# Other start addresses for TensorE's operands, and another order of two token tiles, in a hybrid decoder layer

## The chip, the cores and the metric

The kernel runs on one core of a Trainium2 chip. The metric is the device time of one execution in microseconds (us), the median of the runs.

## The reference

One layer, in float32, on 256 tokens with 16 learned meta tokens put before them (272 rows in all), model width 4096:

```python
h = rmsnorm(x, norm_g)
p = h @ w_in                                   # 4096 -> 16384
q, k, v, g_attn, b, c, hc, z = split(p)        # 8 x 2048 = 16 heads or groups of 128
o = stick_breaking_attention(q, k, v)          # 16 heads, strictly causal
o = group_rmsnorm(o * silu(g_attn))
y = b * short_conv(c * hc)                     # 3 taps
y = group_rmsnorm(y * silu(z))
out = rmsnorm(x + concat([o, y]) @ w_out)      # 4096 -> 4096, meta rows dropped
```

The two large products, with `w_in` (4096 x 16384) and `w_out` (4096 x 4096), make up nearly all of the arithmetic.

## The kernel before, in words

**Split products.** Every float32 operand of the two large products is kept as a pair of float32r values: a rounded part (`h`) and the rest (`lo`). A product is h times h, h times lo and lo times h. ScalarE makes `h` (a cast, L84), VectorE makes `lo` (a subtraction, L85).

**Weights.** They arrive in chunks of 128 partitions x 1024 columns (4 KB a partition), one DMA each on SyncE's queue, into four rotating buffers `raw`; each chunk is split into one of four `wh` and one of four `wl`, up to three steps before TensorE uses it. A chunk holds eight slices of 128 columns for `w_in`, two of 512 or four of 256 for `w_out`.

**Input projection, 128 blocks of 128 output columns.** x stands transposed in `xs`, one tile of four k (k counts 32 groups of 128 channels): for each k a row of 272 tokens of the rounded part and a row of 272 of the rest, one behind the other. The weights' slice is the stationary operand (128 x 128), x is the moving one, and 32 k add up in one PSUM bank. There are three kinds of block, each with its own loop body:

- fused blocks (q, attention gate, b, z; 64 of them): per k a pair, L216 (`lo` with 256 columns of the rounded x) and L218 (`h` with both rows of x, 2 x 256 = 512 columns; the first k has it under L215). The meta tokens are skipped, so a row is read from its 16th token on.
- k and v (32 blocks): per k a trio, L222, L223, L224, each of 272 columns, from the row's beginning; L223 moves the second row, the other two the first.
- c and h of the convolution (32 blocks): the same trio with 258 columns, from the row's 14th token on.

The first unit (16 steps) works on four blocks in turn, two k of each in a step; all later steps work on eight k of one block.

**Mixing.** Attention, convolution, gates and norms of each unit run on VectorE and ScalarE in tasks some steps later; TensorE gets a few small products between blocks. The result, one of 32 mixed channel groups, is split into `mixh` and `mixl` (256 tokens each).

**Output projection.** Here the mixed channels are the stationary operand (128 channels x 128 tokens, so two token tiles) and the weights move: seven blocks of 512 columns with 16 chunks each, then two of 256 with eight. Per channel group m and token tile t there is a trio L471, L472, L473. Each token tile has a PSUM bank of its own. When a block is complete, VectorE and ScalarE add the residual, take squares and multiply by the final gain, per token tile. The last block does token tile 0 first and tile 1 after it; four of its chunks are kept split in tiles `kh` and `kl`.

**Where operands begin.** The pools are filled in a fixed order, so a tile's first byte within its partition follows from the sizes of what lies before it. Counted modulo 256 bytes, before the change the weights (`raw`, `wh`, `wl`) begin at 64 and every slice of them too, the mixed channels at 224, the kept chunks at 224. A row of x is 272 x 4 = 1088 bytes and a k is 2176 bytes, 8.5 times 256, so that x begins at alternating places: in a fused block the first row is read from 32 or 160 (the second from 96 or 224), in k and v blocks the first from 224 or 96 (the second from 32 or 160), in convolution blocks the first from 24 or 152 (the second from 88 or 216); the first of each pair of numbers belongs to an even k, the other to an odd one.

Of the kernel before, what the change touches and what calls it, by code (L numbers as in the profile page):

```python
# [8 lines left out]
F32 = mybir.dt.float32  # L9
F32R = mybir.dt.float32r  # L10
# [5 lines left out]
P = 128  # L16
# [3 lines left out]
META = 16  # L20
L = SEQ + META
HEADS = 16
UNITS = 32
# [3 lines left out]

# Reciprocal square root: an exponent-halving seed, one tuned Newton step, one cubic step.
SEED = float(0x5F1FFFF9)
NA = 2.38924456  # L30
NB = 0.703952253
RS = -0.375 * NB

# Matrix products before the first data; the step at which the rows' statistics begin.
WARM = 10
S0 = 7

# Columns of the packed parameters.
G0, CW0, AG0, CG0, NPAR = 0, 32, 80, 96, 112
# [3 lines left out]
def kernel(ctx, tc, xt, xin, par, fg, w1, w2, out):  # L43
    nc = tc.nc

    const = ctx.enter_context(tc.tile_pool(name="const", bufs=1))
    wp = ctx.enter_context(tc.tile_pool(name="wp", bufs=4))
    wk = ctx.enter_context(tc.tile_pool(name="wk", bufs=1))
    pp = ctx.enter_context(tc.tile_pool(name="pp", bufs=8, space=bass.MemoryType.PSUM))

    def bank(nm):
        return pp.tile([P, 512], F32, tag="bank", name=nm)

    # The tensor engine's clock rises while it works.
    ones = const.tile([P, P], F32, name="ones")
# [7 lines left out]

    # ------------------------------------------------------------ weights
    raws, splits = {}, {}
# [21 lines left out]

    # ------------------------------------------------------------ constants
    ones_r = const.tile([P, P], F32R, name="ones_r")
    nc.scalar.copy(out=ones_r, in_=ones)  # L90
    # Attention weights [query, key]: the second query tile's key tile 1, key tile 0 of both query
    # tiles, then the last 16 keys of each, 32 columns apart.
    za = const.tile([P, 3 * P + 64], F32, name="za")
    nc.vector.memset(za[:, 3 * P:], 0.0)
    # Transposed, [key, query]: key tile 1 (16 queries of the first tile, the second), key tile 0.
    at = const.tile([P, META + 3 * P], F32, name="at")
# [5 lines left out]
    for off in (META, 144 + META + P):  # L102
        # Column c of the diagonal block is a key before query p where c < p.
        nc.gpsimd.affine_select(out=zmask[:, off:off + P], in_=zmask[:, off:off + P],
                                pattern=[[-1, P]], compare_op=ALU.is_gt, fill=NEG,
                                base=0, channel_multiplier=1)
    one = const.tile([P, 1], F32, name="one")
# [5 lines left out]
    def rsqrt_raw(src, n, eps, nm):  # L113
        """u with rsqrt(src + eps) = RS * u."""
        x = wk.tile([P, 272], F32, tag="rx", name=f"rx{nm}", bufs=1)[:, :n]
        y = wk.tile([P, 272], F32, tag="ry", name=f"ry{nm}", bufs=1)[:, :n]
        t = wk.tile([P, 272], F32, tag="rt", name=f"rt{nm}", bufs=1)[:, :n]
        v = nc.vector
        v.tensor_scalar(out=x, in0=src, scalar1=eps, scalar2=None, op0=ALU.add)  # L119
        v.tensor_scalar(out=y.bitcast(I32), in0=x.bitcast(I32), scalar1=-0.5, scalar2=SEED,  # L120
                        op0=ALU.mult, op1=ALU.add)
        v.tensor_tensor(out=t, in0=y, in1=y, op=ALU.mult)
        v.tensor_tensor(out=t, in0=t, in1=x, op=ALU.mult)
        v.scalar_tensor_tensor(out=y, in0=t, scalar=-NA, in1=y, op0=ALU.add, op1=ALU.mult)
        v.scalar_tensor_tensor(out=t, in0=y, scalar=NB * NB, in1=y, op0=ALU.mult, op1=ALU.mult)
        v.tensor_tensor(out=t, in0=t, in1=x, op=ALU.mult)
        v.scalar_tensor_tensor(out=t, in0=t, scalar=-10.0 / 3.0, in1=t, op0=ALU.add, op1=ALU.mult)
        v.scalar_tensor_tensor(out=y, in0=t, scalar=5.0, in1=y, op0=ALU.add, op1=ALU.mult)
        return y

    # ------------------------------------------------------------ mixed channels, split
    mixh, mixl = [], []

    def open_mix():
        sctx.close()
        mixp = ctx.enter_context(tc.tile_pool(name="mixp", bufs=1))
        mixh.extend(mixp.tile([P, SEQ], F32R, name=f"mixh{m}") for m in range(UNITS))
        mixl.extend(mixp.tile([P, SEQ], F32R, name=f"mixl{m}") for m in range(UNITS))

    # ------------------------------------------------------------ steps over weight chunks  # L140
    # Unit 0: two k of all four blocks in a step. Other blocks: eight k of one block.
    steps = [(0, kc) for kc in range(16)]
    for b in range(4, 128):
        steps.extend((b, kc) for kc in range(4))
    n1 = len(steps)
    # w_out: seven blocks of 512 columns, then two of 256.
    for nb in range(7):
# [23 lines left out]
    xp = xctx.enter_context(tc.tile_pool(name="xp", bufs=1, side="right"))  # L171
    xs = [xp.tile([P, 4, 2, L], F32R, name=f"xs{j}") for j in range(8)]
    sctx = ExitStack()
# [8 lines left out]
    def prep_x(k):  # L182
        j, kk = k // 4, k % 4
        g = pt[:, G0 + k:G0 + k + 1]
        nc.scalar.mul(out=xs[j][:, kk, 0, :], in_=xr[j][:, kk, :], mul=g)
        nc.vector.scalar_tensor_tensor(out=xs[j][:, kk, 1, :], in0=xr[j][:, kk, :], scalar=g,
                                       in1=xs[j][:, kk, 0, :].bitcast(F32),
                                       op0=ALU.mult, op1=ALU.subtract)
# [19 lines left out]
    def mm_k(b, k, h, lo):  # L208
        """One k of a block of w_in."""
        ps = psum[b]  # L210
        x = xs[k // 4][:, k % 4]
        first, last = k == 0, k == KC - 1
        if b % 8 in (0, 3, 6, 7):
            if first:
                nc.tensor.matmul(out=ps, lhsT=h, rhs=x[:, :, META:], start=True, stop=False)  # L215
            nc.tensor.matmul(out=ps[:, :SEQ], lhsT=lo, rhs=x[:, 0, META:], start=False, stop=False)  # L216
            if not first:
                nc.tensor.matmul(out=ps, lhsT=h, rhs=x[:, :, META:], start=False, stop=last)  # L218
        else:
            s = 0 if b % 8 < 4 else META - 2  # L220
            o = ps[:, s:L]
            nc.tensor.matmul(out=o, lhsT=h, rhs=x[:, 0, s:], start=first, stop=False)  # L222
            nc.tensor.matmul(out=o, lhsT=h, rhs=x[:, 1, s:], start=False, stop=False)  # L223
            nc.tensor.matmul(out=o, lhsT=lo, rhs=x[:, 0, s:], start=False, stop=last)  # L224
# [15 lines left out]
    def blocks(dst, src, n):  # L240
        """n [128, 128] transposes from one with its 32 x 32 blocks transposed in place."""
        d = dst.rearrange("p (c x) -> p c x", c=n)
        s = src.rearrange("p (c x) -> p c x", c=n)
        for i in range(4):
            for j in range(4):
                o = d[32 * j:32 * j + 32, :, 32 * i:32 * i + 32]
                x = s[32 * i:32 * i + 32, :, 32 * j:32 * j + 32]
                if (i + j) % 2:
                    nc.vector.tensor_copy(out=o, in_=x)
                else:  # L250
                    nc.scalar.copy(out=o, in_=x)  # L251

    def fold(ps, r, nm, tag, width=SEQ):
        """Both halves of a fused block, times the rows' scale."""
        t = wk.tile([P, width], F32, tag=tag, name=f"{tag}{nm}")[:, :SEQ]
        nc.scalar.copy(out=t, in_=ps[:, SEQ:])
        nc.vector.tensor_tensor(out=t, in0=ps[:, :SEQ], in1=t, op=ALU.add)
        nc.vector.tensor_tensor(out=t, in0=t, in1=r, op=ALU.mult)
        return t
# [29 lines left out]
    def head_block(b, e):  # L289
        u = b // 4  # L290
        h = u // 2
# [5 lines left out]
        elif kind == 1:  # L297
# [32 lines left out]
            def trans():  # L330
                y = wk.tile([P, 448], F32, tag="zl", name=f"ya{h}")
                nc.vector.transpose(out=y, in_=za)  # L332
                blocks(at[:, META:], y[:, :3 * P], 3)
                # Only the last 16 queries of a tile see its last 16 keys.
                nc.vector.tensor_copy(out=at[:META, :META], in_=y[96:96 + META, 400:416])
# [93 lines left out]

    # ------------------------------------------------------------ output projection  # L430
    res, fgs, acc, sqs = [], {}, [], []
# [23 lines left out]
    def mm_out(ci, ts):  # L455
        b, kc = steps[ci]
        wh, wl = splits[ci]
        _, n = cols(b)
        nm = 1024 // n
        if kc == 0:  # L460
            for t in ts:
                psum[b, t] = bank(f"mo{b}_{t}")
        for kk in range(nm):
            m = nm * kc + kk
            h = wh[:, kk * n:(kk + 1) * n]
            lo = wl[:, kk * n:(kk + 1) * n]
            for t in ts:
                o = psum[b, t][:, :n]
# [42 lines left out]

    # ------------------------------------------------------------ the program
    load_x(0, 1)
# [21 lines left out]
    for i in range(1 - SPLITS, n_steps):  # L535
        # The last block's kept chunks are split up to four steps earlier.
        ahead = min(4, max(0, i - (n_steps - 16) + 5))
# [95 lines left out]
```

## Time and profile before

| | |
|---|---|
| median of 3 runs | 1894.76 us (1894.72 to 1895.06) |
| span of the profiled execution, first to last instruction | 1893.8 us |
| TensorE (PE) busy | 1880.2 us, 99% |
| weight loads (PEld) busy | 1721.8 us, 91% |
| VectorE (DVE) busy | 1226.0 us, 65% |
| ScalarE (ACT) busy | 952.7 us, 50% |
| DMA queue of the kernel, share of 16 engines | 56.7% |

The span stands for the profiled execution's own time; around it lies the launch, and the median of the runs is 1.0 us above it. "Busy" is the time in which at least one instruction of the engine is under way. TensorE's matmuls are pipelined and overlap in the record, so that a full bar does not say how fast they follow each other; starts of consecutive matmuls do.

### The profile page before, as it was taken

Reading aid. Unit: us, or ns where it says so; the run is one execution under the profiler, and the core shown is the slowest. Engines: PE = TensorE matmul, PEld = TensorE weight load, DVE = VectorE, ACT = ScalarE, POOL = GpSimd, SP = SyncE. Lnnn points to the kernel's source line nnn. Section 1 sums busy time; section 2 is a strip of 40 time slices with the busy share of each in tenths; the row PEclk is TensorE's granted clock in tenths of the full one; section 3 lists DMA queues with packets and bytes.
Section 4 is the critical chain, followed back from the end, with each engine's and each line's share of the span. In section 5 each row is a group of like instructions: output and inputs, shape, how many; then the busy total and the mean of one; then the engine's idle time right before and its main releaser. Section 6 shows DMA issues by size and latency. Waiting matters only on the chain.

```text
span 1893.8 us, 30516 instructions
## 1 busy us (share of the span) xinstructions
PE 1880.2 (99%) x12214; PEld 1721.8 (91%) x12214; DVE 1226.0 (65%) x1904; ACT 952.7 (50%) x1381; POOL 0.7 (0%) x6
## 2 busy tenths in 40 slices
PE   9999999999999999999999999999999999999997
PEld 8999999999999999999999999999999988888887
DVE  8987666766666667676767676767676754555544
ACT  7665454545454545454545454545454543444433
POOL 0000000000000000000000000000000000000000
PEclk9999999999999999999999999999999999999999
DMA  8555555555555555555555555555555586665564
GB/s 307 171 178 186 171 186 172 184 172 185 172 184 173 184 173 184 173 184 173 183 174 183 175 182 175 181 175 181 176 180 176 181 288 195 193 195 192 191 191 165
DMA packets 100510, 352.53 MB, mean 186 GB/s; under 512 B 11280, under 2 KB 12560, under 8 KB 100368
## 3 DMA queue, kind: packets, MB, share of 16 engines
q1 hardware_dynamic: 100368, 350.59, 56.7%
q8 instruction: 95, 1.56, 0.4%
q14 instruction: 47, 0.39, 0.1%
HBM read 346.35 MB, written 4.19 MB: 185 GB/s over the span
## 4 chain that ended last, share of the span: by engine, by line
PE 99%; DMA 0%; DVE 0%; SPq 0%; ACT 0%; issue 0%; DVEq 0%; ACTq 0%
PE mm L218 24%; PE mm L222 13%; PE mm L223 13%; PE mm L224 13%; PE mm L216 13%; PE mo L473 6%; PE mo L472 6%; PE mo L471 6%; PE mm L215 1%; PE z L304 0%; DMA raw<-w 0%; PE po L366 0%; PE po L368 0%; PE po L367 0%; PE z L303 0%; PE ss L277 0%
## 5 line engine op out<-in xcount | busy, mean ns | idle before, releaser
L85 DVE TENSOR_TENSOR wl<-raw,wh 128x1024 fp32r<-128x1024 f32 (+1 forms) x638 | 777.4, 1219 | 452.3 <-ACT wh L84 449.0
L84 ACT CAST wh<-raw 128x1024 fp32r<-128x1024 f32 (+1 forms) x638 | 667.1, 1046 | 778.8 <-PE mm L223 331.0
L218 PE MATMUL mm<-xs,wh 128*128 128x512 f32 x1984 | 698.9, 394 | 0.0
L222 PE MATMUL mm<-xs,wh 128*128 128x258 f32 (+1 forms) x2048 | 590.5, 288 | 1.2 <-ACT wh L84 1.2
L223 PE MATMUL mm<-xs,wh 128*128 128x258 f32 (+1 forms) x2048 | 587.2, 287 | 0.0
L224 PE MATMUL mm<-xs,wl 128*128 128x258 f32 (+1 forms) x2048 | 583.4, 285 | 0.0
L216 PE MATMUL mm<-xs,wl 128*128 128x256 f32 x2048 | 563.3, 280 | 0.3 <-DVE wl L85 0.3
L218 PEld LDWEIGHTS mm<-xs,wh 128*128 128x128 f32 x1984 | 371.7, 187 | 83.9
L223 PEld LDWEIGHTS mm<-xs,wh 128*128 128x128 f32 x2048 | 387.1, 189 | 2.7
L216 PEld LDWEIGHTS mm<-xs,wl 128*128 128x128 f32 x2048 | 384.5, 188 | 4.8 <-DVE wl L85 0.7
L222 PEld LDWEIGHTS mm<-xs,wh 128*128 128x128 f32 x2048 | 384.7, 188 | 2.6 <-ACT wh L84 1.5
L224 PEld LDWEIGHTS mm<-xs,wl 128*128 128x128 f32 x2048 | 386.0, 189 | 0.2
L473 PE MATMUL mo<-wl,mixh 128*128 128x512 f32 (+1 forms) x544 | 205.7, 378 | 0.0
L472 PE MATMUL mo<-wh,mixh 128*128 128x512 f32 (+1 forms) x544 | 203.6, 374 | 0.0
L471 PE MATMUL mo<-wh,mixl 128*128 128x512 f32 (+1 forms) x544 | 202.7, 373 | 0.0
L472 PEld LDWEIGHTS mo<-wh,mixh 128*128 128x128 f32 x544 | 102.1, 188 | 21.8
L471 PEld LDWEIGHTS mo<-wh,mixl 128*128 128x128 f32 x544 | 102.2, 188 | 20.2
L473 PEld LDWEIGHTS mo<-wl,mixh 128*128 128x128 f32 x544 | 102.3, 188 | 19.3
L251 ACT COPY at<-ya 32x96 f32<-32x96 f32 x128 | 34.5, 269 | 12.2 <-DVE ya L332 10.7
L251 ACT COPY vv<-yv 32x64 f32<-32x64 f32 x128 | 31.0, 243 | 1.7
L119 DVE TENSOR_SCALAR rxm<-ss 128x256 f32<-128x256 f32 x32 | 13.6, 424 | 26.2 <-PE ss L277 26.2
L318 DVE SCALAR_TENSOR_TENSOR zs<-zm,zl 128x416 f32<-128x416 f32 x16 | 9.5, 592 | 30.5 <-ACT zl L311 30.4
(141 smaller groups left out, 907.4 us busy)
## 6 DMA issues: line engine op xcount, KB each, us to landing
raw<-w SPq DMA_DIRECT2D x638, 512.0 KB, 3.4
xr<-xt SPq DMA_DIRECT2D x15, 272.0 KB, 6.4
res<-xin SPq DMA_DIRECT2D x14, 256.0 KB, 4.9
out<-res SPq DMA_DIRECT2D x4, 512.0 KB, 3.4
fg<-fg SPq DMA_DIRECT2D x7, 256.0 KB, 4.0
out<-res SPq DMA_DIRECT2D x2, 640.0 KB, 4.8
raw<-w SPq DMA_DIRECT2D x4, 256.0 KB, 4.8
res<-xin SPq DMA_DIRECT2D x4, 128.0 KB, 4.6
```

The costliest lines, as they stand in the source:

```text
L84: nc.scalar.copy(out=h[:, c], in_=t[:, c])
L85: nc.vector.tensor_tensor(out=lo[:, c], in0=t[:, c], in1=h[:, c].bitcast(F32), op=ALU.subtract)
L215: nc.tensor.matmul(out=ps, lhsT=h, rhs=x[:, :, META:], start=True, stop=False)
L216: nc.tensor.matmul(out=ps[:, :SEQ], lhsT=lo, rhs=x[:, 0, META:], start=False, stop=False)
L218: nc.tensor.matmul(out=ps, lhsT=h, rhs=x[:, :, META:], start=False, stop=last)
L222: nc.tensor.matmul(out=o, lhsT=h, rhs=x[:, 0, s:], start=first, stop=False)
L223: nc.tensor.matmul(out=o, lhsT=h, rhs=x[:, 1, s:], start=False, stop=False)
L224: nc.tensor.matmul(out=o, lhsT=lo, rhs=x[:, 0, s:], start=False, stop=last)
L251: nc.scalar.copy(out=o, in_=x)
L471: nc.tensor.matmul(out=o, lhsT=ml, rhs=h, start=m == 0, stop=False)
L472: nc.tensor.matmul(out=o, lhsT=mh, rhs=h, start=False, stop=False)
L473: nc.tensor.matmul(out=o, lhsT=mh, rhs=lo, start=False, stop=m == UNITS - 1)
```

## The change

Five edits, in the diff below. The DMA scratch at the bottom of each partition shrinks from 16384 to 256 bytes. A row of `xs` grows from 272 to 320 elements (1280 bytes, five times 256), of which 272 are written and read as before. Three unused tiles, `pad_w`, `pad_m` and `pad_x`, shift what lies behind them. Counted modulo 256 bytes, the weights and the mixed channels now begin at 128; both rows of every k of x are read from 128 in fused blocks, from 64 in k and v blocks and from 120 in convolution blocks; the kept chunks stay at 224. In `mm_out` the loop over the token tiles stands outside the loop over a chunk's channel groups.

```diff
+XROW = 320
...
+    wp.tile([P, 16], F32, name="pad_w", bufs=1)
     pp = ctx.enter_context(tc.tile_pool(name="pp", bufs=8, space=bass.MemoryType.PSUM))
...
         mixp = ctx.enter_context(tc.tile_pool(name="mixp", bufs=1))
+        mixp.tile([P, 24], F32, name="pad_m")
...
-    xs = [xp.tile([P, 4, 2, L], F32R, name=f"xs{j}") for j in range(8)]
+    xs = [xp.tile([P, 4, 2, XROW], F32R, name=f"xs{j}") for j in range(8)]
+    xp.tile([P, 40], F32, name="pad_x")
...
-        nc.scalar.mul(out=xs[j][:, kk, 0, :], in_=xr[j][:, kk, :], mul=g)
-        nc.vector.scalar_tensor_tensor(out=xs[j][:, kk, 1, :], in0=xr[j][:, kk, :], scalar=g,
-                                       in1=xs[j][:, kk, 0, :].bitcast(F32),
+        nc.scalar.mul(out=xs[j][:, kk, 0, :L], in_=xr[j][:, kk, :], mul=g)
+        nc.vector.scalar_tensor_tensor(out=xs[j][:, kk, 1, :L], in0=xr[j][:, kk, :], scalar=g,
+                                       in1=xs[j][:, kk, 0, :L].bitcast(F32),
...
-        x = xs[k // 4][:, k % 4]
+        x = xs[k // 4][:, k % 4, :, :L]
...
-        for kk in range(nm):
-            m = nm * kc + kk
-            h = wh[:, kk * n:(kk + 1) * n]
-            lo = wl[:, kk * n:(kk + 1) * n]
-            for t in ts:
+        for t in ts:
+            for kk in range(nm):
+                m = nm * kc + kk
+                h = wh[:, kk * n:(kk + 1) * n]
+                lo = wl[:, kk * n:(kk + 1) * n]
                 o = psum[b, t][:, :n]
...
-    nc = bacc.Bacc("TRN2", target_bir_lowering=False, num_devices=1)
+    nc = bacc.Bacc("TRN2", target_bir_lowering=False, num_devices=1, dynamic_dma_scratch_size=256)
```

On TensorE only the output projection's order differs. Its first chunk stood like this before; a row names the line, the PSUM tile (`mo_0` and `mo_1` are the banks of the two token tiles), the moving weights and the stationary channels:

```order
L471 MATMUL mo_0_16171<-wh_16232,mixl_992 128x512
L472 MATMUL mo_0_16171<-wh_16232,mixh_960 128x512
L473 MATMUL mo_0_16171<-wl_16233,mixh_960 128x512
L471 MATMUL mo_1_16172<-wh_16232,mixl_992 128x512
L472 MATMUL mo_1_16172<-wh_16232,mixh_960 128x512
L473 MATMUL mo_1_16172<-wl_16233,mixh_960 128x512
L471 MATMUL mo_0_16171<-wh_16232,mixl_993 128x512
L472 MATMUL mo_0_16171<-wh_16232,mixh_961 128x512
L473 MATMUL mo_0_16171<-wl_16233,mixh_961 128x512
L471 MATMUL mo_1_16172<-wh_16232,mixl_993 128x512
```

The bank alternates after every trio. The same place after the change, on TensorE, with the lines' new numbers and the tiles' new ones:

```order
L476 MATMUL mo_0_16174<-wh_16235,mixl_995 128x512
L477 MATMUL mo_0_16174<-wh_16235,mixh_963 128x512
L478 MATMUL mo_0_16174<-wl_16236,mixh_963 128x512
L476 MATMUL mo_0_16174<-wh_16235,mixl_996 128x512
L477 MATMUL mo_0_16174<-wh_16235,mixh_964 128x512
L478 MATMUL mo_0_16174<-wl_16236,mixh_964 128x512
L476 MATMUL mo_1_16175<-wh_16235,mixl_995 128x512
L477 MATMUL mo_1_16175<-wh_16235,mixh_963 128x512
L478 MATMUL mo_1_16175<-wl_16236,mixh_963 128x512
L476 MATMUL mo_1_16175<-wh_16235,mixl_996 128x512
```

Two channel groups now follow each other in one bank before the other token tile's bank is written. All other rows of TensorE, and all rows of the other engines, keep their places.

## Rows read from the trace of the kernel before

**Rows 1.** The profile page: the span, TensorE's busy time, and the chain that ended last.

```profile
span 1893.8 us, 30516 instructions
...
PE 1880.2 (99%) x12214; PEld 1721.8 (91%) x12214; DVE 1226.0 (65%) x1904; ACT 952.7 (50%) x1381; POOL 0.7 (0%) x6
...
PE 99%; DMA 0%; DVE 0%; SPq 0%; ACT 0%; issue 0%; DVEq 0%; ACTq 0%
```

**Rows 2.** Windows: stretch, each engine's busy time and count, granted clock, DMA share, GB/s.

```profile
60.00:1548.00 1488.00, 1488.00 (x10214) 1390.22 (x10213) 1002.64 (x1639) 772.94 (x1161) 0.00 (x0) 1.00 0.56 181
```

**Rows 3.** Groups by line and shape: count | busy us, mean ns of one | idle before.

```profile
L218 PE MATMUL mm<-xs,wh 128*128 128x512 f32 x1984 | 698.9, 394 | 0.0
...
L222 PE MATMUL mm<-xs,wh 128*128 128x272 f32 x1024 | 298.7, 292 | 1.2 <-ACT wh L84 1.2
...
L222 PE MATMUL mm<-xs,wh 128*128 128x258 f32 x1024 | 291.9, 285 | 0.0
...
L471 PE MATMUL mo<-wh,mixl 128*128 128x512 f32 x448 | 175.6, 392 | 0.0
```

**Rows 4.** Timeline of TensorE, a k block: start us, duration, line; first of each trio.

```profile
496.16 0.29 PE L222 MATMUL mm<-xs,wh 128*128 128x272 f32 x1
...
496.53 0.29 PE L222 MATMUL mm<-xs,wh 128*128 128x272 f32 x1
...
496.92 0.29 PE L222 MATMUL mm<-xs,wh 128*128 128x272 f32 x1
...
497.29 0.29 PE L222 MATMUL mm<-xs,wh 128*128 128x272 f32 x1
```

**Rows 5.** The same in a convolution block: two trios, then the ninth.

```profile
450.03 0.28 PE L222 MATMUL mm<-xs,wh 128*128 128x258 f32 x1
...
450.39 0.28 PE L222 MATMUL mm<-xs,wh 128*128 128x258 f32 x1
...
452.94 0.28 PE L222 MATMUL mm<-xs,wh 128*128 128x258 f32 x1
```

**Rows 6.** The same in a fused block: the first of each pair.

```profile
462.12 0.28 PE L216 MATMUL mm<-xs,wl 128*128 128x256 f32 x1
...
462.48 0.28 PE L216 MATMUL mm<-xs,wl 128*128 128x256 f32 x1
...
462.83 0.28 PE L216 MATMUL mm<-xs,wl 128*128 128x256 f32 x1
...
463.17 0.28 PE L216 MATMUL mm<-xs,wl 128*128 128x256 f32 x1
...
463.52 0.28 PE L216 MATMUL mm<-xs,wl 128*128 128x256 f32 x1
```

**Rows 7.** The same in the output projection, 512 columns: one trio and the next start.

```profile
1599.99 0.39 PE L471 MATMUL mo<-wh,mixl 128*128 128x512 f32 x1
1600.22 0.39 PE L472 MATMUL mo<-wh,mixh 128*128 128x512 f32 x1
1600.45 0.40 PE L473 MATMUL mo<-wl,mixh 128*128 128x512 f32 x1
1600.69 0.39 PE L471 MATMUL mo<-wh,mixl 128*128 128x512 f32 x1
```

**Rows 8.** The same in its last block, kept chunks: four trios between the rows.

```profile
1861.06 0.28 PE L471 MATMUL mo<-kh,mixl 128*128 128x256 f32 x1
...
1862.49 0.28 PE L471 MATMUL mo<-kh,mixl 128*128 128x256 f32 x1
```

**Rows 9.** The same in the first unit: a fused block's matmul, then another block's.

```profile
13.39 0.39 PE L218 MATMUL mm<-xs,wh 128*128 128x512 f32 x1
13.62 0.29 PE L222 MATMUL mm<-xs,wh 128*128 128x272 f32 x1
```

**Rows 10.** Timeline of the end: the last matmul.

```profile
1882.52 0.28 PE L473 MATMUL mo<-wl,mixh 128*128 128x256 f32 x1
```

## The prediction, made before the change was run

> **What bounds the kernel now.** I read the page first. TensorE (PE) is busy for 1880.2 of 1893.8 us, and the chain that ended last lies on PE for 99% of the span [rows 1]. A busy PE need not be PE at its peak, so the next question is whether it waits or merely streams slowly. The windows answer it: from 60 to 1548 us PE is busy for 1488.00 of 1488 us at a granted clock of 1.00, which is the 2.4 GHz level, while VectorE works 1002.64 us, ScalarE 772.94 us and the DMA engines have a share of 0.56 [rows 2]. No other engine is near its limit, nothing is waited for, and the clock cannot rise. What is left is the pitch: the time from the start of one matmul to the start of the next. Almost the whole span is that pitch times the counts: 2048 fused pairs (a 512 and a 256; 1984 of the 512 stand under this line, the first k of each block under another), 1024 trios of 272 columns, 1024 trios of 258, and 448 trios of 512 in the output projection, which ends with some of 256 [rows 3]. After the last matmul starts at 1882.52 us the chain runs a tail of some 11 us [rows 10], which the change leaves alone.
>
> So I read the timeline in each family, only for starts (it prints 0.01 us).
>
> Key and value blocks, 272 columns: one k is a trio. The starts of the first matmul of each trio lie 0.37, 0.39, 0.37 us apart [rows 4]. At one column per cycle of 2.4 GHz a trio would take 3 x 272 / 2.4 = 340 ns; it takes 380 on average. The alternation is what the reader is to see. Instructions, shapes, PSUM bank and weights' place modulo 256 bytes are the same from trio to trio. What alternates is where x begins: a row pair of x is 2 x 272 x 4 = 2176 bytes, 8.5 times 256, so every second k begins 128 bytes further modulo 256. In the loop, then, a start address is worth some 20 ns a trio, 6 to 7 ns a matmul.
>
> Convolution blocks, 258 columns: 0.36 for the first trio, and 2.91 us for eight, 0.364 on average, against 322 ns of columns [rows 5]. The alternation is weaker, 0.36 and 0.37.
>
> Fused blocks: four pairs take 0.36, 0.35, 0.34 and 0.35 us [rows 6]; 0.35 on average, against 768 columns or 320 ns.
>
> Output projection: 0.23, 0.23 and 0.24 in a trio, 0.70 in all, against 640 ns of columns [rows 7]. Its blocks of 256 columns take 1.43 us for four trios, 0.358 each, against 320 ns [rows 8].
>
> **The change part by part.** It adds no instruction and removes none. Four things happen.
>
> *The small scratch, the three pads, the wider x rows.* The order on VectorE, ScalarE, GpSimd and SyncE is the old one row for row, so these cost no time by themselves. What hides any slower write is the slack in [rows 2]: VectorE is busy for 67% and ScalarE for 52% of that stretch, so VectorE's work could lengthen by almost half before it set the pace. I cost it at nothing. Were that cover gone, the splits of the weights would be late, and PE would wait for them.
>
> *The starts of PE's operands.* Before, weights begin 64 bytes past a multiple of 256, mixed channels 224, and x at places that alternate. After, weights and mixed channels begin at 128, and every x row has the same place: 128 where the meta tokens are skipped (fused blocks), 64 for k and v, 120 for the convolution. No row of before has these pairs of starts, so each family is bounded by its own rows:
>
> - k and v: either all trios take 0.37 or all take 0.39. Against the mean of 0.38 that is 1024 x 0.01 = 10 us less or more. In distance from weights to x modulo 256, the trios of 0.37 have 160 for the first and third matmul and 224 for the second, those of 0.39 have 32 and 96. After, it is 64 - 128, which is 192, between the two of the 0.37 trios. I take -10 us.
> - Convolution: 0.36 or 0.37 against 0.364, so -4 or +6 us. The distance becomes 248, between 216 and 24 (both in the trios of 0.37 rather than 0.36) but next to the fused blocks' 224; the rows don't decide, and I take 0.
> - Fused: all pairs at the fastest step, 0.34, give 2048 x 0.01 = 20 us less; all at 0.36 give 20 us more. The distance becomes 0 for both rows of the 512 and for the 256. Before, a pair at 32 (distance 224) holds the 0.34 step and also the 0.36, so I can't read a clean class. What is certain is that the 512's second row no longer begins elsewhere than the first. I take half of the gain, -10 us.
> - Output projection: distance 96 before (moving 64, stationary 224), 0 after. [Rows 8] is a run at distance 0: kept weights and mixed channels both begin 224 past, and the pitch of 0.358 / 3 = 0.119 us has the same excess over its columns (0.119 - 0.107 = 13 ns) as a k or v matmul. So distance 0 is neither cured nor ill there. I take 0 for the starts.
>
> *The order in the output projection.* It changes the PSUM bank every six matmuls (every twelve in the 256-wide blocks) instead of every three. The third matmul's pitch is 0.24 where the others have 0.23 [rows 7], and the bank changes right after it. If the change of bank is what costs 0.01, half of 448 disappear: -2.2 us. Against it: in the first unit, where the blocks alternate, a 512 is followed by another block's matmul, so in another bank, after 0.23 [rows 9], no later than without a change. I take -1. Nobody waits longer: a chunk is split whole before its first matmul, so the order inside it moves no wait, and token tile 0 of a block ends six matmuls before tile 1 instead of three, which gives its eviction more room.
>
> *Sum.* -10 + 0 - 10 + 0 - 1 = -21 us. The profiled execution spans 1893.8 us, and the median of the runs is 1.0 us above it, 1894.8; the terms are the same for both, so the forecast is 1894.8 - 21 = 1874 us. With every term at its better end it is -10 - 4 - 20 - 2 = -36, 1859 us; I give the forecast's own range as 1859 to 1890.
>
> **The rivals.** *Deeper: the excess itself goes.* Every family has 12 to 20 ns a matmul over its columns, whatever its parity, and in these families no moving operand of before starts at a multiple of 128 bytes; after, those of the fused blocks and of nearly all of the output projection do, and so do the weights. If that excess is largely the price of a stray start, halving it in the fused blocks (350 - 320 = 30 ns a pair, 15 x 2048 = 31 us), in the 512-wide trios (60 ns, 30 x 448 = 13 us) and leaving k, v and convolution at the forecast's -10 gives 1840 us; halving it in k, v and convolution too (20 ns x 2048 trios = 41 us, in place of the -10) gives 1810 us. For it: it is by far the largest amount of time that PE spends on anything but columns. Against it: weights, x and mixed channels at six different places all pay nearly the same. The Trainium skill ("TensorE: Matmul & The Clock Gate", Wait — 56ns, not 53.3ns?) puts the pitch of a warm matmul at its columns and 2.5 ns more, 215.7 ns for 512; by that figure in all families my estimate would be some 1750 us, and the rows, with 0.23 to 0.24, do not agree with it before the change.
>
> *Nothing moves.* The alternation could belong to something that the change keeps, such as the parity of the weights' slices in a chunk, and each family would keep its mean: 1895 us. The other engines do not care, and the new order alone is worth 2 us at most. The Trainium skill says it in "SBUF — State Buffer", Who interferes with whom: PE reads the moving and the stationary operand through two independent ports and never waits for anyone, so start places would change nothing. The alternation of 0.37 and 0.39 at full clock with nothing waited for [rows 4] speaks against that rule here.
>
> *Slower: equal places collide.* Fused blocks and output projection now begin both operands at the same place. If two reads that begin together get in each other's way at every matmul, the fused pair goes to its longest step, 0.36 (+20 us), and all three of an output trio to 0.24 (0.72, +0.02 x 448 = +9 us); with k and v still 10 us better that is +19, 1914 us. It decides as soon as the fused pair's mean passes 0.355, which eats what k and v give. Against it stand [rows 8], at distance 0 and no slower than the rest.
>
> **How the numbers follow.** Forecast (1859 to 1890): 0.42. Deeper (below 1859): 0.28. Nothing moves (1891 to 1898): 0.12. Slower: 0.18. A change of 0.2% (3.8 us) is about what a measurement of this kernel can tell from none. The deeper case reaches from 1859 down to about 1800 and lower; cutting at 1812 leaves out less than 0.1. The slower case reaches to 1914 and beyond; cutting at 1902 leaves out about 0.1. So 1812 to 1902. Faster: 0.42 + 0.28 = 0.70; same 0.12; slower 0.18.
>
> **What the profile of after would show.** Granted clock and stalls as now; the k and v trios with one step in place of two (right: 0.37; wrong: 0.39 or still alternating); fused pairs with one step (0.345 expected; 0.36 is the collision; 0.335 or less the deeper case); convolution trios at 0.36 to 0.37; output trios at 0.69 to 0.70, where a 0.24 only after every sixth matmul would put it on the bank, and after every third on something else. The prediction is wrong if the steps still alternate, if a family lands outside its two values of before, or if PE begins to wait for the split weights.

## The result, and the profile after

The changed kernel takes 1873.79 us (median of four runs, 1873.31 to 1874.08) against 1894.82 us: a ratio of 0.9889, 95% interval 0.9875 to 0.9903, so 21 us or 1.1% less. The forecast of 1874 was met almost to the digit, but by terms that are partly wrong and cancel; the rest of this document is about that.

The page after, with the span, the engines and the chain, as in [rows 1]:

```profile
span 1871.5 us, 30516 instructions
...
PE 1859.1 (99%) x12214; PEld 1707.0 (91%) x12214; DVE 1224.7 (65%) x1904; ACT 953.6 (51%) x1381; POOL 0.7 (0%) x6
...
PE 99%; DMA 0%; DVE 0%; SPq 0%; ACT 0%; issue 0%; DVEq 0%; ACTq 0%
```

The window of [rows 2], from 60 to 1548 us:

```profile
60.00:1548.00 1488.00, 1488.00 (x10262) 1385.76 (x10261) 1006.36 (x1643) 778.09 (x1166) 0.00 (x0) 1.00 0.55 183
```

TensorE is as full as before at the same clock, and nothing new is waited for; in the same 1488 us it begins 10262 matmuls instead of 10214. The gain is pitch alone. The timeline of the k block of [rows 4], three trios and the ninth:

```profile
491.02 0.29 PE L227 MATMUL mm<-xs,wh 128*128 128x272 f32 x1
...
491.39 0.28 PE L227 MATMUL mm<-xs,wh 128*128 128x272 f32 x1
...
491.76 0.29 PE L227 MATMUL mm<-xs,wh 128*128 128x272 f32 x1
...
493.98 0.29 PE L227 MATMUL mm<-xs,wh 128*128 128x272 f32 x1
```

The alternation of 0.37 and 0.39 is gone: eight trios take 2.96 us, 0.370 each. The convolution block of [rows 5], first, second and eighth trio:

```profile
445.32 0.28 PE L227 MATMUL mm<-xs,wh 128*128 128x258 f32 x1
...
445.68 0.28 PE L227 MATMUL mm<-xs,wh 128*128 128x258 f32 x1
...
447.82 0.28 PE L227 MATMUL mm<-xs,wh 128*128 128x258 f32 x1
```

Seven trios take 2.50 us, 0.357 each, against 0.364. The fused block of [rows 6], the first of each pair:

```profile
456.95 0.28 PE L221 MATMUL mm<-xs,wl 128*128 128x256 f32 x1
...
457.31 0.28 PE L221 MATMUL mm<-xs,wl 128*128 128x256 f32 x1
...
457.67 0.28 PE L221 MATMUL mm<-xs,wl 128*128 128x256 f32 x1
...
458.01 0.28 PE L221 MATMUL mm<-xs,wl 128*128 128x256 f32 x1
```

Still steps of 0.36, 0.36, 0.34, although every pair now begins at the same place. And the output projection of [rows 7]:

```profile
1600.09 0.39 PE L476 MATMUL mo<-wh,mixl 128*128 128x512 f32 x1
1600.32 0.39 PE L477 MATMUL mo<-wh,mixh 128*128 128x512 f32 x1
1600.54 0.39 PE L478 MATMUL mo<-wl,mixh 128*128 128x512 f32 x1
1600.77 0.39 PE L476 MATMUL mo<-wh,mixl 128*128 128x512 f32 x1
```

0.68 us a trio in place of 0.70. Adding up the pitch of all matmuls of a family in the two traces gives where the 22.3 us between the two spans went (the medians differ by 21.0: the traced execution of after is the fastest of its four, and its span lies 2.3 us under their median, that of before 1.0 us under its own):

| family | before us | after us | difference | forecast |
|---|---|---|---|---|
| k and v, 272 columns | 392.0 | 382.8 | -9.2 | -10 |
| convolution, 258 | 373.1 | 367.6 | -5.5 | 0 |
| fused, 512 and 256 | 719.2 | 720.5 | +1.3 | -10 |
| output, 512 | 313.6 | 304.7 | -8.9 | -1 |
| output, 256 | 45.9 | 45.9 | 0 | 0 |
| all other matmuls of TensorE | 37.6 | 37.7 | +0.1 | 0 |

### The profile page after: what moved, and what is told of

Read it like the earlier page. It is cut to its first block, busy times and chain, and to the rows that moved or that the text cites. A ratio compares the mean times of both kernels' runs of the same rounds, so it can differ in the third digit from the quotient of the medians.

```text
span 1871.5 us, 30516 instructions
## 1 busy us (share of the span) xinstructions
PE 1859.1 (99%) x12214; PEld 1707.0 (91%) x12214; DVE 1224.7 (65%) x1904; ACT 953.6 (51%) x1381; POOL 0.7 (0%) x6
## 4 chain that ended last, share of the span: by engine, by line
PE 99%; DMA 0%; DVE 0%; SPq 0%; ACT 0%; issue 0%; DVEq 0%; ACTq 0%
PE mm L223 25%; PE mm L227 13%; PE mm L229 13%; PE mm L228 13%; PE mm L221 13%; PE mo L478 6%; PE mo L477 6%; PE mo L476 6%; PE mm L220 1%; PE z L309 0%; PE po L371 0%; DMA raw<-w 0%; PE po L373 0%; PE po L372 0%; PE z L308 0%; PE ss L281 0%
## 5 line engine op out<-in xcount | busy, mean ns | idle before, releaser
L478 PE MATMUL mo<-wl,mixh 128*128 128x512 f32 (+1 forms) x544 | 201.5, 370 | 0.0
```

Of the source, the lines that this page charges most:

```text
L478: nc.tensor.matmul(out=o, lhsT=mh, rhs=lo, start=False, stop=m == UNITS - 1)
```

## The experiments

Two theories. **D**: the pitch of a family depends on the distance, modulo 256 bytes, from where the stationary operand begins to where the moving one begins. **A** (called M in two expectations, for the moving operand alone): what counts is each operand's own place, for instance a multiple of 128. And for the output projection a third: the order of the token tiles did it. The diffs are against the changed kernel unless the text says otherwise. Pitches with three decimals below are means over all pairs or trios of a family in that run's trace, without those that contain a wait.

**The order alone** (the kernel before, with the new loops and nothing else):

```diff
+        for t in ts:
+            for kk in range(nm):
...
-            for t in ts:
```

> The kernel before with the new order of the token tiles alone; all starts as before. If the order (the change of PSUM bank after every trio) cost the 0.24 step, the 512-wide output trio falls from 0.70 to about 0.68 and the time by about 9 us, to 1886. If the starts did it, the trio stays at 0.70 and the time at 1894.8.

1894.78 us, ratio 1.0000 (0.9991 to 1.0009). The timeline of its output projection:

```profile
1611.67 0.39 PE L473 MATMUL mo<-wh,mixl 128*128 128x512 f32 x1
1611.90 0.39 PE L474 MATMUL mo<-wh,mixh 128*128 128x512 f32 x1
1612.13 0.40 PE L475 MATMUL mo<-wl,mixh 128*128 128x512 f32 x1
1612.37 0.39 PE L473 MATMUL mo<-wh,mixl 128*128 128x512 f32 x1
1612.60 0.39 PE L474 MATMUL mo<-wh,mixh 128*128 128x512 f32 x1
1612.83 0.40 PE L475 MATMUL mo<-wl,mixh 128*128 128x512 f32 x1
1613.07 0.39 PE L473 MATMUL mo<-wh,mixl 128*128 128x512 f32 x1
```

The 0.24 still stands after every third matmul, although the bank now changes after every sixth. It does not belong to the bank, and the order is worth nothing. **The starts alone**, with the old order:

```diff
-        for t in ts:
-            for kk in range(nm):
...
+            for t in ts:
```

> The changed kernel with the old order of the token tiles. If the starts did it all: output trios 0.68, time 1873.8 as with the whole change. If the order made the output projection's part: output trios 0.70, time about 1883.

1873.96 us, ratio 0.9889 (0.9872 to 0.9905), with output trios of 0.680: the starts did all of it.

**The weights alone** (the kernel before with the weights at 128; a larger `pad_m` keeps the mixed channels at 224, and the scratch is shrunk for room):

```diff
+    wp.tile([P, 16], F32, name="pad_w", bufs=1)
...
+        mixp.tile([P, 48], F32, name="pad_m")
```

> The kernel before with the weights moved from 64 to 128 alone; x (rows of 272, alternating) and mixed channels (224) begin where they began. Theory D (the distance from the stationary to the moving start counts): the k and v trios, whose distances become 96, 160, 96 and 224, 32, 224, lose their 0.37 and 0.39 and both come near 0.38. Theory M (the moving operand's own place counts): x has not moved, so 0.37 and 0.39 stay. Output trios (moving at 128, distance 160): 0.68 by M if a start at a multiple of 128 is what helped, open by D.

1893.74 us, ratio 0.9993 (0.9984 to 1.0003). Its k block:

```profile
494.94 0.29 PE L226 MATMUL mm<-xs,wh 128*128 128x272 f32 x1
...
495.31 0.29 PE L226 MATMUL mm<-xs,wh 128*128 128x272 f32 x1
...
495.69 0.28 PE L226 MATMUL mm<-xs,wh 128*128 128x272 f32 x1
```

x has not moved, and the two kinds of trio went from 0.373 and 0.385 to 0.371 and 0.380: the weights' place matters too, so the moving place alone is not it. But D's forecast, that the alternation goes, was met only in half: 0.37 and 0.38 remain. Output trios took 0.703 with the moving operand at 128, so a moving start at a multiple of 128 is not what helped.

**All three operands moved together** by 128:

```diff
-    wp.tile([P, 16], F32, name="pad_w", bufs=1)
+    wp.tile([P, 48], F32, name="pad_w", bufs=1)
...
-    xp.tile([P, 40], F32, name="pad_x")
+    xp.tile([P, 8], F32, name="pad_x")
```

> The changed kernel with weights, x and mixed channels all moved on by 128 bytes modulo 256, so that all distances stay. Theory D: every family as in the changed kernel (k and v 0.371, convolution 0.359, fused 0.352, output 0.680), 1873.8 us. Theory M with a period of 256: families shift, k and v by up to 0.02 a trio, so up to 20 us more or less. M with a period of 128 is not told from D here.

1874.32 us, ratio 0.9891 (0.9877 to 0.9906). The k block, first and ninth trio, and an output trio:

```profile
492.22 0.28 PE L227 MATMUL mm<-xs,wh 128*128 128x272 f32 x1
...
495.18 0.28 PE L227 MATMUL mm<-xs,wh 128*128 128x272 f32 x1
...
1598.25 0.39 PE L476 MATMUL mo<-wh,mixl 128*128 128x512 f32 x1
...
1598.93 0.39 PE L476 MATMUL mo<-wh,mixl 128*128 128x512 f32 x1
```

2.96 us for eight trios and 0.68, and the others agree too: 0.357 and 0.352. Except for the kept chunks, which stay at 224, every start is another, every distance the same, and so is every mean pitch.

**Distances scanned.** Four runs move x and the mixed channels against the weights, which stay at 128; the edit is the size of two pads, `pad_x` and `pad_m`, shown for 128; they are 24 and 8 elements for 64, 56 and 40 for 192, 48 and 32 for 224:

```diff
-        mixp.tile([P, 24], F32, name="pad_m")
+        mixp.tile([P, 56], F32, name="pad_m")
...
-    xp.tile([P, 40], F32, name="pad_x")
+    xp.tile([P, 8], F32, name="pad_x")
```

> The changed kernel with x moved on by 64 bytes (distances from the weights: fused 64, k and v 0, convolution 56) and the mixed channels moved back by 64 (output distance 64). Theory D (the distance of the two operands' starts modulo 256 sets the pitch): the output trio leaves 0.680, toward the 0.700 seen at 96; fused pair leaves 0.352. Theory A (what counts is that each operand by itself begins at a multiple of 128): output 0.700 because the stationary start has lost it; k and v improve on 0.370 because x gains it.

> The changed kernel with x moved on by 128 and the mixed channels moved back by 128 (distances: fused 128, k and v 64, convolution 120, output 128). Theory A: every operand keeps its place modulo 128, so all families stay: output 0.680, fused 0.352, k and v 0.370, convolution 0.357, 1873.8 us. Theory D: output leaves 0.680 for 0.700 or more, as at 96 and 160, and the others move too, by up to 0.015 a trio.

> Distances: fused 192, k and v 128, convolution 184, output 192. Theory D: k and v leave 0.370, which they had at 192; fused and output take a new value, for D open between 0.680 and 0.703 for the output. Theory A: output 0.700 (stationary start off a multiple of 128), k and v as good as 0.370 or better, since x begins at 0.

> Distances: fused 224, k and v 160, convolution 216, output 224. In the kernel before, a fused 256-column matmul took 0.116 at 224 and 0.120 at 96, so by theory D the fused pair falls below 0.352, to about 0.345 (2048 x 0.007 = 14 us); k and v stay near 0.372, the value of trios at 160 and 224; the output is open. Theory A: all off multiples of 128, output 0.700, fused 0.350 as before.

One run each: 1883.97, 1891.99, 1896.69 and 1885.94 us. The one at 128 separates the theories. Its k block, first and ninth trio, and its output, first and fifth:

```profile
495.04 0.29 PE L227 MATMUL mm<-xs,wh 128*128 128x272 f32 x1
...
498.08 0.29 PE L227 MATMUL mm<-xs,wh 128*128 128x272 f32 x1
...
1610.17 0.40 PE L476 MATMUL mo<-wh,mixl 128*128 128x512 f32 x1
...
1612.96 0.39 PE L476 MATMUL mo<-wh,mixl 128*128 128x512 f32 x1
```

All operands have their places modulo 128, which by A leaves everything alone, and k and v take 0.380, the output 0.697: 18 us are lost. A is out. At 192 the kernel is no faster than before, with an order and a row width that are those of the change. At 224 my expectation for the fused pair (0.345) failed; it took 0.352. So did D's expectation that the fused pair leaves 0.352 at 64, and A's that k and v do no worse than 0.370 with x at multiples of 128: the fused pair takes 0.351 to 0.353 at 64, 128 and 192, and k and v take 0.376 in the run at 64 and 0.380 in the run at 192.

The run at 192 also holds two distances in one block. The kept chunks begin at 224 in every kernel, the mixed channels at 192 here, so the kept weights lie at a distance of 32 and the other weights at 192. In the last block of 256 columns, the first of each trio: from `wh`, four trios later the first from `kh`, and four trios after that:

```profile
1871.33 0.28 PE L476 MATMUL mo<-wh,mixl 128*128 128x256 f32 x1
...
1872.69 0.28 PE L476 MATMUL mo<-kh,mixl 128*128 128x256 f32 x1
...
1874.09 0.28 PE L476 MATMUL mo<-kh,mixl 128*128 128x256 f32 x1
```

0.340 a trio at 192 and 0.350 at 32, and 0.350 is what the other weights take in the run at 32. Over all runs the kept chunks take what the last row of the table below has for their distance, within 1 ns at 0, 32, 64, 96 and 224; at 128 and 160 they are 3 ns faster, which D does not explain.

**x alone**, and **the mixed channels alone**, in the kernel before, both with the weights at 64. The first gives x rows of 320 and a pad of 56; the second is one pad:

```diff
+XROW = 320
...
+    xp.tile([P, 56], F32, name="pad_x")
```

> The kernel before with x alone changed: rows of 320 elements, begun at 64 in fused blocks, 0 in k and v, 56 in the convolution; weights stay at 64, mixed channels at 224, the order stays old. The input projection then has the changed kernel's distances (0, 192, 248) at places 64 bytes lower, not one of them the changed kernel's. Theory D: fused 0.352, k and v 0.370, convolution 0.357, output 0.700 as before; about 1883 us. A rival by which the distances count only with starts at multiples of 128: k and v back near 0.38, about 1893.

```diff
+        mixp.tile([P, 24], F32, name="pad_m")
```

> The kernel before with the mixed channels alone moved from 224 to 64 by one pad of 24 elements: output distance 0 with both starts at 64; nothing else changes. Theory D: the 512-wide output trio goes from 0.700 to 0.680, 448 x 0.020 = 9 us, 1886; the input projection as before. The rival that wants multiples of 128: 0.700 and 1894.8. Together with the run on x alone the two parts should add up to the whole change (12 + 9 = 21).

The first takes 1880.71 us (ratio 0.9925, 0.9910 to 0.9940), the second 1885.95 (0.9953, 0.9936 to 0.9969). The k block of the first (first and ninth trio), and an output trio of the second:

```profile
491.49 0.28 PE L225 MATMUL mm<-xs,wh 128*128 128x272 f32 x1
...
494.45 0.28 PE L225 MATMUL mm<-xs,wh 128*128 128x272 f32 x1
```

```profile
1609.66 0.39 PE L474 MATMUL mo<-wh,mixl 128*128 128x512 f32 x1
...
1610.34 0.39 PE L474 MATMUL mo<-wh,mixl 128*128 128x512 f32 x1
```

2.96 us for eight trios, so 0.370, and 0.68, at places 64 bytes from those of the change. So the mixed channels' one pad is worth 9 us, and x 14. Added up that is 23, two more than the whole change: the fused pair takes 0.350 here and 0.352 there at the same distance of 0, 3 us that D does not explain. The trace of the change shows where they lie. Two of its fused blocks, first and ninth pair of each:

```profile
372.23 0.28 PE L221 MATMUL mm<-xs,wl 128*128 128x256 f32 x1
...
375.01 0.28 PE L221 MATMUL mm<-xs,wl 128*128 128x256 f32 x1
...
383.33 0.28 PE L221 MATMUL mm<-xs,wl 128*128 128x256 f32 x1
...
386.17 0.28 PE L221 MATMUL mm<-xs,wl 128*128 128x256 f32 x1
```

2.78 and 2.84 us for eight pairs, at the same distance in the same kernel. Of its 62 fused blocks after the first unit 18 run at 0.347 a pair and 44 at 0.354; with x alone changed it is 32 and 30. The 14 blocks more at the lower level, 32 pairs each, are the 3 us. So the distance alone does not fix a block's pitch, and the averages in this document are mixtures of such levels where a family has two; what puts a block on one of them is not shown.

**Distance 32**, and then **a version put together from the scan**, x at 32 and mixed channels at 0:

```diff
-    xp.tile([P, 40], F32, name="pad_x")
+    xp.tile([P, 32], F32, name="pad_x")
```

> The changed kernel at a distance of 32 in fused blocks and output (k and v 224, convolution 24). Theory D says only that the families leave the changed kernel's values: k and v were at 0.3795 with distances 224, 32, 224 and should be above 0.370; the output lies between 0.680 (at 0) and 0.687 (at 64) if the curve is smooth. If it is under 0.680, there is a better place than the change's.

> The changed kernel with pad_x of 32 elements in place of 40: x 32 bytes further, so the input projection has the distances of the run at 32 (fused 32, k and v 224, convolution 24) and the output projection keeps distance 0. Theory D takes each family by itself: fused 0.347 (from 0.352, 2048 x -0.005 = -10 us), k and v 0.377 (from 0.370, 1024 x 0.007 = +7), convolution 0.356 (-1), output 0.680; about 1870 us, some 4 below the changed kernel. If the families' pitches depend on each other or on more than the distances: no better than 1873.8.

At 32 (where the mixed channels have a pad of 16 elements as well) one run took 1879.55 us; the output went to 0.700, so its curve is not smooth, but the fused pair fell to 0.347. The combination takes 1871.68 us (1871.62 to 1871.81), ratio 0.9878 (0.9862 to 0.9894). Its fused block and its k block, first and ninth each:

```profile
457.37 0.28 PE L221 MATMUL mm<-xs,wl 128*128 128x256 f32 x1
...
460.14 0.28 PE L221 MATMUL mm<-xs,wl 128*128 128x256 f32 x1
...
491.16 0.29 PE L227 MATMUL mm<-xs,wh 128*128 128x272 f32 x1
...
494.17 0.29 PE L227 MATMUL mm<-xs,wh 128*128 128x272 f32 x1
```

Fused pairs of 0.346 and k and v trios of 0.376 in these blocks, 0.347 and 0.377 on average, and the output at 0.680: each family took the value that it had at its distance in another run. The version lies 2.1 us under the changed kernel, half of what the families promised and within the two ratios' intervals; its runs and those of the changed kernel don't overlap, but I call it no more than a small gain.

Mean pitch in ns by distance (k, v and fused from runs in which all rows of x begin at one place; 96 from the kernel before, 160 in the output from the run with the weights alone; the last row without the kept chunks):

| distance | 0 | 32 | 64 | 96 | 128 | 160 | 192 | 224 |
|---|---|---|---|---|---|---|---|---|
| k and v trio | 376 | - | 380 | - | 380 | 371 | 370 | 377 |
| fused pair | 350 to 352 | 347 | 352 | - | 351 | - | 353 | 352 |
| output trio, 512 | 680 | 700 | 687 | 700 | 697 | 703 | 700 | 700 |
| output trio, 256 | 360 | 350 | 353 | 360 | 359 | 355 | 341 | 355 |

## Why the prediction came out right, step by step

- *What bounds the kernel* held: pitch at full clock, no waits, and other engines with room. Reading the alternation of [rows 4] as the price of a start address was the step that carried the forecast. The experiments show that starts have a price: no instruction and no order differs between the kernels of the scan and the version put together from it, and they range from 1872 to 1897 us. An alternating step alone does not show it, though: in the run at 224 all k and v trios lie at one distance, 160, and their steps of 0.368 and 0.372 still take turns.
- *k and v*, -10: measured -9.2, by the mechanism given. 192 lies between 160 and 224, and took 0.370. That reading between two neighbours was lucky, though: with both rows of x at 224 a trio takes 0.377.
- *Convolution*, 0: measured -5.5, just outside the bounds of -4 to +6. The rows of before did not bound the family. Nor is it enough to say that 216 and 24 are poor distances: the trios that had both take 0.365 on average before, but 0.360 with all rows at 216 and 0.356 with all at 24. Why the mixture costs more stays open.
- *Fused*, -10: measured +1.3. The step that failed is "I take half of the gain". I had read the 0.34 step as a state that a steady start might keep. But the steps of [rows 6] were not those of x's two places: in the trace of before 0.355, 0.354, 0.348 and 0.343 repeat every four pairs, while x's place repeats every two. After, at one single place, 0.346, 0.358 and 0.356 repeat every three in most blocks. The mean hardly depends on the distance (0.350 to 0.353), except at 32 (0.347), which the change doesn't have.
- *Output projection, starts*, 0: measured -8.9. The step that failed is "distance 0 is neither cured nor ill there", drawn from [rows 8]. It was true of 256 columns, which take 0.360 a trio at 96 and, within 1 ns, at 0 (the kept chunks before, the others after), and it did not carry over to 512, which fell from 0.700 to 0.680.
- *Output projection, order*, -1: measured 0. The 0.24 in [rows 7] went with the distance, not with the bank; [rows 9] had said so.
- The sum was right because the fused term (11 us too good) and the output and convolution terms (8 and 5.5 us too poor) cancelled. That it met the time to 0.2 us is luck.
- *The signs of being wrong* that the prediction set itself: two of the three came. The fused steps still alternate, and the convolution (0.357) and the 512-wide output trios (0.680) landed outside their values of before. Only the third, PE waiting for the split weights, did not. The account of k and v held; that of the other families did not.
- *The rivals.* "Nothing moves" is refuted. What the prediction drew from the rule of the Trainium skill ("SBUF — State Buffer", Who interferes with whom), that start places would change nothing, does not hold here: 18 us between distances 0 and 128 at full clock with nothing waited for. Whether the two reads get in each other's way, or something else depends on the distance, the runs don't show. "Equal places collide" is refuted as stated, since the 512-wide output trios are at their best at equal places; the fused blocks did get 1.3 us worse, and the 256-wide output trios are at their worst there (0.360, as at 96). "Deeper" is refuted: starts at multiples of 128 do not remove the excess over columns. Where both operands now begin at one, it fell from 60 to 40 ns in the 512-wide output trios, but stays at 40 in the 256-wide ones and goes from 30 to 32 in the fused pairs. In k and v, whose x begins elsewhere, it fell from 39 to 30, in the convolution from 40 to 35.

Left open: why a distance costs what it does. The runs show the dependence, not what reads meet where. Within a family all stationary tiles begin at the same place modulo 256, so the distances to the matmul's own weights and to those of the next one are equal here, and no run tells which of them counts. Also open is what puts a fused block at 0.347 or 0.354 with distance 0.

## What to carry to other kernels

When TensorE is full at full clock, compare the pitch of equal matmuls within one loop: a step that alternates may be the price of an address that padding can move. See first whether it repeats as often as the address does (in k and v it did, in the fused blocks not), and don't take the steps of before as bounds; the convolution and the output projection landed outside theirs. Change the distance between the two operands' starts for one family of matmuls at a time and read each family's pitch on its own, since the best distance differs by shape, and a total can be right for wrong reasons. Don't carry a pitch from one width to another.

## What was not expected of the hardware

- The pitch of back-to-back float32r matmuls with a new stationary operand each depended on the distance between the two operands' starts modulo 256 bytes: 680 to 703 ns for three of 512 columns, 341 to 360 for three of 256, 370 to 380 for three of 272.
- The best of the distances run depends on the width: 0 for 512 columns, where 256 are at their worst (0.360 a trio); 192 for 256 columns (0.341), where 512 take 0.700.
- At one distance, in one kernel, fused blocks ran at either of two pitches, 0.347 or 0.354 a pair, each kept through a whole block.
- Moving both operands by 128 bytes changed no family's mean pitch by a nanosecond; moving one of them by 128 cost 17 ns a trio in the output projection.
